# Convolution: the low parts of fourteen weights as a sign-turned cast plus an accumulating transfer

## The chip, the cores and the metric

The kernel runs on one core of a Trainium2 chip. Five engines work side by side, each through its own queue of instructions in a fixed order: TensorE (PE, matmuls), VectorE (DVE), ScalarE (ACT), GpSimd (POOL) and SyncE (SP, which here only issues transfers). They wait for each other and for transfers through semaphores. The metric is the device time in microseconds (us); three runs of the kernel before gave 1223.39, 1224.14 and 1225.11, so its time is their median, 1224.14 us.

## The reference, cut to what matters

Two decoder layers over 512 tokens of width 1024 in float32. The first layer begins with a causal convolution module, and only this stage is touched by the change:

```python
u = rms_norm(h, conv_norm_g)
a = u @ w_pw1 + b_pw1                               # 1024 -> 2048
u = a[..., :1024] * sigmoid(a[..., 1024:])          # value half, gate half
u = depthwise_conv(u, dw_w, width=31) + dw_b        # causal, per channel
u = silu(layer_norm(u, ln_g, ln_b))
h = h + u @ w_pw2 + b_pw2
# after it: the SwiGLU FFN, and h + sigmoid(rms_norm(h) @ ple_w_gate) * (p @ ple_w_proj);
# then the second layer with differential attention in place of the convolution
```

## The kernel before, in words

**Split operands.** To keep float32 precision, each operand of a matmul is split into a high part (`hi`, a rounded cast) and a low part (`lo = raw - hi`). A product is three matmuls, `mm3` (L182 to L185): low weight times high input first, then high times low, then high times high. A weight tile is 128 x 1024 (512 KB) and serves as eight 128 x 128 pieces, so half a chunk (one accumulator) takes 8 x 3 = 24 matmuls.

**Weights.** `weight` fetches a raw tile into `wraw`, a ring of two (L166, issued by SP), casts it on ACT into `whi` (L171) and subtracts on an engine `eng` into `wlo` (L173); `whi` and `wlo` are rings of four tiles, so two pairs. A weight's raw tile is free again once its last reader is done. I call the weights w0, w1, ... in the order in which they are fetched: w0 to w3 belong to chunks 0 and 1; w4 and w5 are gate and value of chunk 2, w6 and w7 of chunk 3, and so on to w14 and w15 of chunk 7. Two more, `pw`, serve the projections of `p` that fill PE after the convolution (`factor`, L617 and before). The low parts of w4 to w15 are DVE's, those of `pw` are POOL's.

**The loop over eight chunks of 128 channels.** For chunk c, PE makes the gate half, then the value half. Chunk 0 and 1 start before the norm is known: the row factors `rb` of the norm are multiplied in afterwards. `rb` comes from PE transposes (L263), is copied by ACT (L240), and DVE multiplies gate and value by it (L557, L559), which empties the PSUM accumulators, of which there are four (`mm`). ACT applies the sigmoid (L558), DVE joins both (L563, L575). The depthwise taps are made in two ways:

- Chunks 1, 3, 5, 6 ("phased"): the result is stored to DRAM (`pi`, L389, SP), read back rearranged by four transfers (`C`, L393, SP), multiplied on PE with diagonal matrices (L422, 64 matmuls of 128 x 128 per chunk, diagonals `D` and `C` loaded by SP at L406 and L412), copied out by ACT (L435), stored (`po`, L437, issued by ACT for chunks 1 and 3) and read back by four transfers (`B`, L440, SP), and finished on DVE (L449).
- Chunks 0, 2, 4, 7: some taps are products on ACT (L475, into four tiles in turn) added by POOL (L476), the others run on DVE (L487), with a last sum on DVE (L492).

Then the moments for the layer norm are formed (L515, L520, L523, L595) and turned by PE transposes (L256) and a spread (L263). Chunk 0's ones-matmul (L513) gives a per-token shift that is taken off early.

**What sets the order.** The kernel is written as one program and a scheduler fixes each engine's order statically; a few steps are tied by hand (`issue_after`). An instruction that waits holds up all that stands behind it on the same engine, and SP's and POOL's transfers too.

Of the kernel before, what the change touches and what calls it, by code (L numbers as in the profile page):

```python
# [13 lines left out]
F32R = mybir.dt.float32r  # L14
AF = mybir.ActivationFunctionType
ALU = mybir.AluOpType
# [43 lines left out]
BEHIND = (6,)  # L60
# [34 lines left out]
def trunk(ctx, tc, xT, pT, wts, diag, dww, vec, rel, lamv, out):  # L95
    nc = tc.nc
    V, A, G, T = nc.vector, nc.scalar, nc.gpsimd, nc.tensor
# [7 lines left out]
    def sb(shape, tag, bufs, dt=F32):  # L105
        uid[0] += 1
        return pool.tile(shape, dt, tag=tag, name=f"{tag}_{uid[0]}", bufs=bufs)
# [17 lines left out]
    def col(name, i=0):  # L125
        a, _ = VEC[name]
        return vt[:, a + i : a + i + 1]
# [22 lines left out]
    def opened(homes=None, raw_home=None):  # L150
        i = wnext[0]
        wnext[0] += 1
        if raw_home:
            raw = sb([P, 2, S], raw_home, 1).rearrange("p a s -> p (a s)")
        else:
            raw = sb([P, 1024], "wraw", 2)
        if homes:
            hi, lo = (sb([P, 2, S], t, 2, F32R).rearrange("p a s -> p (a s)") for t in homes)
        else:
            hi, lo = (sb([P, 1024], t, 4, F32R) for t in ("whi", "wlo"))  # L160
        return i, raw, hi, lo

    def fetch(w, cut, behind=None):
        i, raw, _, _ = w
        with tc.issue_after(behind.ins) if behind else nullcontext():
            loaded[0] = nc.sync.dma_start(raw[:, cut], wts[i, :, cut])  # L166

    def parts(w, cut, eng=V, after=None, behind=None):
        _, raw, hi, lo = w
        with tc.issue_after(behind.ins) if behind else nullcontext():  # L170
            last_cast[0] = A.copy(hi[:, cut], raw[:, cut])  # L171
        with tc.issue_after(after.ins) if after else nullcontext():
            eng.tensor_tensor(lo[:, cut], raw[:, cut], f(hi[:, cut]), ALU.subtract)  # L173

    def weight(n=1024, home=None, load_behind=None, **how):
        w, cut = opened(home), slice(0, n)
        fetch(w, cut, load_behind)
        parts(w, cut, **how)
        return w[2:]
# [90 lines left out]
    pairs = [(w1[2:], w0[2:]), (w3[2:], w2[2:])]  # L270
# [28 lines left out]
    def pfeatures(layer, parts, behind=None):  # L299
        for k, (hi, lo) in enumerate(parts):  # L300
            if layer == 0:
                if k == 0:
                    two = sb([P, 2, S], "B7", 1)
                    with tc.issue_after(loaded[0].ins):
                        nc.sync.dma_start(two.rearrange("p a s -> p (a s)"), pT[layer])
                raw = two[:, k]
            else:
                raw = sb([P, 1024], "wraw", 2)[:, :S]
                nc.sync.dma_start(raw, pT[layer, :, k * S : (k + 1) * S])
            with tc.issue_after(behind.ins) if behind else nullcontext():  # L310
                A.copy(hi, raw)
            (G if layer == 0 else V).tensor_tensor(lo, raw, f(hi), ALU.subtract)
        return parts
# [25 lines left out]
    phase_load = [None]  # L339
# [3 lines left out]
    def half(w, behind={}):  # L343
        acc = mm()
        held = nullcontext
        for k in range(NC):
            if k in behind:
                held = partial(tc.issue_after, behind[k].ins)
            with held():
                mm3(acc, wpart(w, k), norm.u[k], k == 0, k == NC - 1)  # L350
        return acc

    def first_halves(wa, wg):
        pg, pa = mm(), mm()
        for k in range(NC):
            (uh, ul), last = norm.u[k], k == NC - 1
            for acc, w in ((pg, wg), (pa, wa)):
                wh, wl = wpart(w, k)
                T.matmul(acc, wh, uh, start=k == 0, stop=False)
                T.matmul(acc, wl, uh, start=False, stop=False)  # L360
            for acc, w in ((pg, wg), (pa, wa)):
                T.matmul(acc, wpart(w, k)[0], ul, start=False, stop=last)
        return pg, pa

    def wt(c, j):
        return dwt[:, c * KW + j : c * KW + j + 1]
# [4 lines left out]
    def pe_taps(c):  # L371

        acc = accs[c] = sc() if c < NC - 2 else mm()
        if c in PHASED:
            return phased_taps(c, acc)
        for j in range(PE_TAPS[c]):
            if j % 4 == 0:
                n = min(4, PE_TAPS[c] - j)
                dg = sb([P, 2, 4, P], "C5", 2)[:, 0]
                with tc.issue_after(outs[NC - 3].ins):  # L380
                    nc.sync.dma_start(dg[:, :n], diag[TAPS.index((c, j)), :, :n])
            if j == 0:
                T.matmul(acc, ident, shrow, start=True, stop=False)
            last_tap[0] = T.matmul(acc, dg[:, j % 4], ups[c][:, j : j + S], start=False, stop=(j == PE_TAPS[c] - 1))

    def phased_in(c, src):

        d = dram.tile([P, S], F32, tag=f"pi{c}", name=f"pi{c}")
        nc.sync.dma_start(d, src)  # L389
        xs = ups[c] = sb([P, NPH, LEAD + P], "C1", 2)  # L390
        G.memset(xs[:, :, :LEAD], 0.0)
        for i in range(NPH):
            phase_load[0] = nc.sync.dma_start(  # L393
                xs[i * FG : (i + 1) * FG, :, LEAD:],
                bass.AP(d.tensor, d.offset + i * P, [[S, FG], [FG * S, NPH], [1, P]]),
            )
# [138 lines left out]
    for c in range(NC):  # L535
        wa, wg = pairs[c]
        if c == 0:
            pg, pa = first_halves(wa, wg)
            norm.factors()
            rb = norm.rows()  # L540
            pairs.append((weight(), weight())[::-1])
            pair_loads.append(loaded[0])
            ph = pfeatures(0, [(sb([P, S], t, 2, F32R), sb([P, S], t, 2, F32R)) for t in ("wth", "wtl")], norm.spread)
        if 1 < c < NC - 1:
            pairs.append((weight(), weight(load_behind=phase_load[0] if c + 1 in BEHIND else None))[::-1])
            pair_loads.append(loaded[0])
        if c > 0:
            pg = half(wg)
            if c - 1 not in PHASED:
                pe_taps(c - 1)  # L550
            pa = half(wa, {1: norm.last_column, 6: norm.last_row} if c == 1 else {})
            if c - 1 in PHASED and c < NC - 2:
                pe_taps(c - 1)
            if c == NC - 1:
                pe_taps(c - 2)
        tg, ta = big(), big()
        V.tensor_tensor(tg, pg, rb, ALU.mult)  # L557
        A.activation(tg, tg, AF.Sigmoid, bias=col("b_pw1", 8 + c))  # L558
        V.tensor_tensor(ta, pa, rb, ALU.mult)  # L559
        if c in PHASED:  # L560
            up = big()
            phases, tok = "p (r n) -> p n r", "p (n r) -> p n r"
            V.scalar_tensor_tensor(  # L563
                up.rearrange(phases, r=NPH), ta.rearrange(tok, r=NPH), col("b_pw1", c),
                tg.rearrange(tok, r=NPH), ALU.add, ALU.mult,
            )
            phased_in(c, up)
            rest = rests[c] = sb([P, 2, P], "rest", 2)[:, :, : P - LAGS]
            old = up.rearrange("p (r n) -> p r n", r=NPH)[:, :, : P - LAGS]
            A.activation(rest, old[:, 2:], AF.Copy, scale=wt(c, 0))  # L570
            V.scalar_tensor_tensor(rest[:, 0], old[:, 3], wt(c, 1), rest[:, 0], ALU.mult, ALU.add)
        else:
            up = ups[c] = sb([P, S + PAD], "C0", 2)
            G.memset(up[:, :PAD], 0.0)
            V.scalar_tensor_tensor(up[:, PAD:], ta, col("b_pw1", c), tg, ALU.add, ALU.mult)  # L575
        if c == NC - 1:
            other_taps(c - 2)
            pe_taps(c - 1)
        if c > 0 and c != NC - 2:
            other_taps(c - 1)  # L580
        if c == 1:
            moments(0)
        elif c > 3:
            moments(c - 3)
# [36 lines left out]
            held.append(copy)  # L621
        pp.append(o)

    pw = [weight(eng=G), weight(eng=G)]
    vs = sb([P, P // 2], "v8", 2)[:, :12]
    for m in range(4):
        factor(last_tap, bank=(mm, mm, mm, sc)[m])
# [566 lines left out]
    for m in range(NC):  # L1194
        if m % 4 == 0:
            w = weight()
# [154 lines left out]
```

## Time and profile before

| | |
|---|---|
| median of three runs | 1224.14 us |
| the profiled execution's own time | 1225.47 us |
| its span (first to last instruction) | 1223.7 us |
| PE busy in the span | 1215.3 us, 99% |
| DVE / ACT / POOL busy | 897.1 / 623.2 / 279.3 us |
| transfers issued by SP, ACT (q1, q10) / by POOL (q0) | 139.0 MB / 16.78 MB |

The profiled execution is one run, 1.33 us above the median. A row of a group reads: line, engine, operation, output<-inputs, shapes, count, then the busy time and the mean of one in ns, then the engine's idle time just before and what ended most of it. In rows of a timeline the first two numbers are the start and the length in us, and the square bracket tells what the engine had waited for. A row of transfers has the size of each and the median time from issue to landing. A name such as `wlo<-wraw,whi` gives output and inputs without buffer numbers.

### The profile page before, as it was taken

The page shows a single profiled execution, that of the slowest core. Times are in us where ns is not written, and L with a number is a line of the kernel's source. Part 1 is how long each engine was busy: PE and PEld are TensorE (multiplying, and loading weights), DVE is VectorE, ACT ScalarE, POOL GpSimd, SP SyncE. Part 2 cuts the span into 40 slices and gives each one's busy share as a digit, 9 for nine tenths or more (in the row PEclk, how much of TensorE's full clock was granted, in tenths as well). Part 3 has the DMA queues.
Part 4 walks back from the last instruction along what each step waited for, and adds up shares of the span by engine and source line. Part 5 has one row for each costly group of instructions (what it writes and reads, how often), then busy time and mean ns, then how long its engine had stood idle before and what let it go on. Part 6 is the DMA issues. An engine that isn't in the chain of part 4 may idle for free.

```text
span 1223.7 us, 18446 instructions
## 1 busy us (share of the span) xinstructions
PE 1215.3 (99%) x7080; PEld 1072.7 (88%) x7080; DVE 897.1 (73%) x1442; ACT 623.2 (51%) x1039; POOL 279.3 (23%) x238
## 2 busy tenths in 40 slices
PE   9999999999999999999999999999999999999998
PEld 7888788898999899888888989888898999899887
DVE  6999957965698458668668879647865687568668
ACT  6764645432355235446566779635442355235443
POOL 0879421000000000042626544131000000000120
PEclk9999999999999999999999999999999999999999
DMA  8655232663567444243222214412654577353241
GB/s 285 216 177 157 93 121 71 187 165 111 125 170 185 141 106 123 84 145 96 76 92 78 78 55 128 138 59 79 182 163 122 136 173 190 105 138 94 78 139 69
DMA packets 60056, 156.96 MB, mean 128 GB/s; under 512 B 6336, under 2 KB 11200, under 8 KB 59968
## 3 DMA queue, kind: packets, MB, share of 16 engines
q1 hardware_dynamic: 53632, 136.20, 34.9%
q0 software_dynamic: 4608, 16.78, 8.3%
q10 hardware_dynamic: 1728, 2.80, 0.8%
q8 instruction: 55, 0.90, 0.3%
q14 instruction: 33, 0.27, 0.1%
HBM read 150.52 MB, written 4.19 MB: 126 GB/s over the span
## 4 chain that ended last, share of the span: by engine, by line
PE 88%; DVE 5%; DMA 3%; issue 1%; POOL 1%; ACT 1%; SPq 0%; DVEq 0%; POOLq 0%; ACTq 0%
PE mm L183 23%; PE mm L184 23%; PE mm L185 23%; PE tp L185 2%; PE tp L184 2%; PE tp L183 2%; PE sc L184 2%; PE sc L185 2%; PE sc L183 2%; PE mm L1119 1%; DVE wlo L173 1%; DMA C<-in_wts 1%; POOL wk L476 1%; DVE sc L487 1%; DMA wraw<-in_wts 1%
## 5 line engine op out<-in xcount | busy, mean ns | idle before, releaser
L183 PE MATMUL mm<-A,wlo 128*128 128x512 f32 (+1 forms) x816 | 277.0, 342 | 0.5 <-DVE wlo L775 0.5
L184 PE MATMUL mm<-A,whi 128*128 128x512 f32 (+1 forms) x816 | 276.8, 340 | 0.5 <-DVE A L198 0.5
L185 PE MATMUL mm<-A,whi 128*128 128x512 f32 (+1 forms) x816 | 276.9, 340 | 0.0
L171 ACT CAST whi<-wraw 128x1024 fp32r<-128x1024 f32 (+2 forms) x142 | 143.4, 1019 | 206.3 <-PE mm L185 88.1
L173 DVE TENSOR_TENSOR wlo<-wraw,whi 128x1024 fp32r<-128x1024 f32 (+2 forms) x135 | 171.7, 1275 | 54.5 <-ACT whi L171 54.4
L183 PEld LDWEIGHTS mm<-A,wlo 128*128 128x128 f32 x816 | 154.8, 190 | 18.1 <-PE sc L185 0.6
L184 PEld LDWEIGHTS mm<-A,whi 128*128 128x128 f32 x816 | 154.8, 190 | 17.7 <-DVE A L198 0.9
L185 PEld LDWEIGHTS mm<-A,whi 128*128 128x128 f32 x816 | 154.8, 190 | 16.6
L184 PE MATMUL mm<-B,whi 128*128 128x512 f32 (+1 forms) x384 | 147.5, 385 | 0.0
L185 PE MATMUL mm<-B,whi 128*128 128x512 f32 (+1 forms) x384 | 147.4, 385 | 0.0
L183 PE MATMUL mm<-B,wlo 128*128 128x512 f32 (+1 forms) x384 | 145.3, 386 | 0.0
L782 POOL DMA_DIRECT2D C<-in_wts x32 | 27.9, 873 | 506.3 <-DVE h L893 134.8
L224 POOL TENSOR_TENSOR acc<-acc,wk 128x512 f32<-128x512 f32 x34 | 55.8, 1640 | 215.3 <-ACT wk L222 107.4
L185 PEld LDWEIGHTS mm<-B,whi 128*128 128x128 f32 x384 | 72.1, 188 | 14.4
L183 PEld LDWEIGHTS mm<-B,wlo 128*128 128x128 f32 x384 | 72.2, 188 | 13.9
L184 PEld LDWEIGHTS mm<-B,whi 128*128 128x128 f32 x384 | 72.2, 188 | 13.7
L184 PE MATMUL mm<-wlo,A 128*128 128x512 f32 (+1 forms) x224 | 81.6, 367 | 0.0
L183 PE MATMUL mm<-whi,A 128*128 128x512 f32 (+1 forms) x224 | 80.9, 366 | 0.0
L185 PE MATMUL mm<-whi,A 128*128 128x512 f32 (+1 forms) x224 | 80.4, 362 | 0.0
L893 DVE TENSOR_TENSOR h<-mm,h 128x512 f32<-128x512 f32 x48 | 32.9, 687 | 63.5 <-PE mm L185 63.5
L250 POOL TENSOR_TENSOR r<-v,mhalf 128x8 f32<-128x8 f32 (+1 forms) x30 | 45.3, 1511 | 123.3 <-DVE v L248 122.5
L476 POOL TENSOR_TENSOR wk<-wk,C 128x512 f32<-128x512 f32 x43 | 63.4, 1479 | 13.5 <-ACT C L475 10.8
(322 smaller groups left out, 2749.6 us busy)
## 6 DMA issues: line engine op xcount, KB each, us to landing
wraw<-in_wts SPq DMA_DIRECT2D x161, 512.0 KB, 3.7
C<-in_wts SPq DMA_DIRECT2D x32, 512.0 KB, 4.5
C<-in_wts POOLq DMA_DIRECT2D x32, 512.0 KB, 6.0
bias<-in_wts SPq DMA_DIRECT2D x32, 256.0 KB, 3.3
wraw<-in_wts SPq DMA_DIRECT2D x16, 384.0 KB, 3.1
D<-in_diag SPq DMA_DIRECT2D x18, 256.0 KB, 4.9
C<-in_diag SPq DMA_DIRECT2D x15, 256.0 KB, 5.6
h<-in_xT SPq DMA_DIRECT2D x8, 256.0 KB, 5.2
```

The lines of the kernel that those rows point to most:

```text
L171: last_cast[0] = A.copy(hi[:, cut], raw[:, cut])
L173: eng.tensor_tensor(lo[:, cut], raw[:, cut], f(hi[:, cut]), ALU.subtract)
L183: T.matmul(acc, al, bh, start=first, stop=False)
L184: T.matmul(acc, ah, bl, start=False, stop=False)
L185: return T.matmul(acc, ah, bh, start=False, stop=last)
L224: self.last = eng.tensor_tensor(self.acc, self.acc, sq, ALU.add)
L250: last_pow[0] = G.tensor_tensor(r[:, :n], v[:, :n], mhalf[:, :n], ALU.pow)
L476: last_pool[0] = G.tensor_tensor(pacc, pacc, pr, ALU.add)
L487: last_sum = V.scalar_tensor_tensor(sum_, tap(j), wt(c, j), sum_, ALU.mult, ALU.add)
L782: nc.gpsimd.dma_start(q, wts[i + 2].rearrange("p (a s) -> p a s", a=2), accum_op=ALU.add)
L893: V.tensor_tensor(h[m], acc, h[m], ALU.add)
L1119: T.matmul(o, wt[:, k * P : (k + 1) * P], val[hd, k], start=(k == 0), stop=(k == qb))
```

## The change

For w4 to w15 and the two `pw` weights the subtract is replaced. ACT casts the raw tile into `whi` as before, and then writes `-hi` into `wlo`; POOL issues a transfer that reads the raw weight a second time from DRAM and adds it onto `wlo` as it lands, so `wlo = -hi + raw`. w0 to w3 and all later weights keep their subtract.

```diff
@@ def parts(w, cut, eng=V, after=None, behind=None):
             last_cast[0] = A.copy(hi[:, cut], raw[:, cut])
+        if eng is None:
+            A.activation(lo[:, cut], hi[:, cut], AF.Copy, scale=-1.0)
+            nc.gpsimd.dma_start(lo[:, cut], wts[w[0], :, cut].bitcast(F32R), accum_op=ALU.add)
+            return
         with tc.issue_after(after.ins) if after else nullcontext():
             eng.tensor_tensor(lo[:, cut], raw[:, cut], f(hi[:, cut]), ALU.subtract)
@@ for c in range(NC), c == 0:
-            pairs.append((weight(), weight())[::-1])
+            pairs.append((weight(eng=None), weight(eng=None))[::-1])
@@ 1 < c < NC - 1:
-            pairs.append((weight(), weight(load_behind=phase_load[0] if c + 1 in BEHIND else None))[::-1])
+            pairs.append((weight(eng=None), weight(eng=None, load_behind=phase_load[0] if c + 1 in BEHIND else None))[::-1])
@@ after the loop
-    pw = [weight(eng=G), weight(eng=G)]
+    pw = [weight(eng=None), weight(eng=None)]
```

Since the scheduler orders the program anew, other instructions move with it, all of them in the convolution stage. The line numbers of the changed kernel are higher by 4 from L175 on; its sign-turned cast is L173, its accumulating transfer L174.

On ACT, around the copy of the row factors `rb`. Before; `whi_269`, `whi_275`, `whi_425` are w4, w5, w6, and `wth`, `wtl` the split `p`:

```order
L171 CAST whi_269<-wraw_268 128x1024
L171 CAST whi_275<-wraw_274 128x1024
L240 COPY rb_261<-tp_262 128x512
L311 CAST wth_280<-B_72_284 128x512
L311 CAST wtl_282<-B_72_284 128x512
L171 CAST whi_425<-wraw_424 128x1024
L558 ACT_TABLE_LOAD
```

The change, with w4, w5 and w6 now 269, 276 and 427, and their low parts 270, 277 and 428:

```order
L171 CAST whi_269<-wraw_268 128x1024
L173 ACTIVATE wlo_270<-whi_269 128x1024
L171 CAST whi_276<-wraw_275 128x1024
L173 ACTIVATE wlo_277<-whi_276 128x1024
L171 CAST whi_427<-wraw_426 128x1024
L173 ACTIVATE wlo_428<-whi_427 128x1024
L244 COPY rb_261<-tp_262 128x512
L315 CAST wth_282<-B_72_286 128x512
L315 CAST wtl_284<-B_72_286 128x512
L562 ACT_TABLE_LOAD
```

The cast of w6 stood behind the `rb` copy and stands ahead of it now, followed by its sign-turned cast. On SP, w6's raw tile has likewise moved, from behind four diagonals (`D`) to ahead of them.

On POOL, between the norm's power (`r_59`) and chunk 0's adds (`wk_367`, then `wk_369`). Before:

```order
L250 TENSOR_TENSOR r_59_259<-v_58_257,mhalf_71 128x4
L312 TENSOR_TENSOR wth_281<-B_72_284,wth_280 128x512
L312 TENSOR_TENSOR wtl_283<-B_72_284,wtl_282 128x512
L476 TENSOR_TENSOR wk_367<-wk_367,C_85_369 128x512
L476 TENSOR_TENSOR wk_367<-wk_367,C_86_372 128x512
L476 TENSOR_TENSOR wk_367<-wk_367,C_87_375 128x512
L476 TENSOR_TENSOR wk_367<-wk_367,C_88_378 128x512
L476 TENSOR_TENSOR wk_367<-wk_367,C_89_381 128x512
L476 TENSOR_TENSOR wk_367<-wk_367,C_90_384 128x512
```

The change (`wlo_435` is the low part of w7):

```order
L174 DMA wlo_270<-in_wts 128x1024
L174 DMA wlo_277<-in_wts 128x1024
L254 TENSOR_TENSOR r_59_259<-v_58_257,mhalf_71 128x4
L174 DMA wlo_428<-in_wts 128x1024
L316 TENSOR_TENSOR wth_283<-B_72_286,wth_282 128x512
L316 TENSOR_TENSOR wtl_285<-B_72_286,wtl_284 128x512
L480 TENSOR_TENSOR wk_369<-wk_369,C_85_371 128x512
L480 TENSOR_TENSOR wk_369<-wk_369,C_86_374 128x512
L480 TENSOR_TENSOR wk_369<-wk_369,C_87_377 128x512
L480 TENSOR_TENSOR wk_369<-wk_369,C_88_380 128x512
L480 TENSOR_TENSOR wk_369<-wk_369,C_89_383 128x512
L174 DMA wlo_435<-in_wts 128x1024
```

w7's accumulating transfer stands behind five of chunk 0's adds. Those of the next weights follow between the adds of chunks 0 and 2; w10's stands ahead of the third to fifth add of chunk 2 (`C_133` to `C_135` in the change), and ACT's copy of chunk 1's taps (L439) stands behind the product that takes the tile which the add of `C_135` frees.

On PE, chunk 1's taps (`sc_486`, in the change `sc_490`). Before, they stand inside the gate half of chunk 3 (w6, `wlo_426`):

```order
L185 MATMUL mm_564<-A_37_153,whi_425 128x512
L422 MATMUL sc_486<-C_82_358,D_105_487 128x128 x4
L422 MATMUL sc_486<-C_82_358,D_106_489 128x128 x4
L422 MATMUL sc_486<-C_82_358,D_107_491 128x128 x4
L422 MATMUL sc_486<-C_82_358,D_108_493 128x128 x4
L422 MATMUL sc_486<-C_82_358,C_109_495 128x128 x8
L422 MATMUL sc_486<-C_82_358,C_110_498 128x128 x8
L183 MATMUL mm_564<-A_39_157,wlo_426 128x512
```

The change: inside the value half (w7, `wlo_435`), behind ten of its matmuls:

```order
L187 MATMUL mm_596<-A_35_145,wlo_435 128x512
L426 MATMUL sc_490<-C_82_360,D_105_491 128x128 x4
L426 MATMUL sc_490<-C_82_360,D_106_493 128x128 x4
L426 MATMUL sc_490<-C_82_360,D_107_495 128x128 x4
L426 MATMUL sc_490<-C_82_360,D_108_497 128x128 x4
L426 MATMUL sc_490<-C_82_360,C_109_499 128x128 x8
L426 MATMUL sc_490<-C_82_360,C_110_502 128x128 x3
L517 MATMUL tp_421<-B_94_398,ones_70 128x512
L426 MATMUL sc_490<-C_82_360,C_110_502 128x128 x5
L188 MATMUL mm_596<-A_36_146,whi_434 128x512
```

The order counts each of these float32 matmuls once; the profile shows 64 for a chunk's 32. They moved back by some 20 matmuls, and the ones-matmul of chunk 0 went in among them. Chunk 3's taps likewise moved, from behind chunk 4's value half to behind six matmuls of chunk 5's gate half.

## The prediction

> **What bounds the kernel now.** I read the page's totals first, then the conv stage (the first 140 us) by windows, since the diff touches only weights of that stage, and last what TensorE (PE) waited for.
>
> ```profile
> span 1223.7 us, 18446 instructions
> PE 1215.3 (99%) x7080; PEld 1072.7 (88%) x7080; DVE 897.1 (73%) x1442; ACT 623.2 (51%) x1039; POOL 279.3 (23%) x238
> ```
>
> PE is busy 99% of the span. The windows show the stage of the change (columns: length; busy time of PE, PEld, DVE, ACT, POOL; granted clock; share of the DMA engines; GB/s):
>
> ```profile
> 20.00:136.70 116.70, 115.58 (x631) 97.84 (x630) 108.93 (x133) 66.60 (x97) 89.38 (x64) 1.00 0.57 187
> 20.00:30.00 10.00, 10.00 (x48) 7.94 (x47) 5.23 (x8) 3.14 (x5) 1.18 (x2) 1.00 0.86 303
> 30.00:45.00 15.00, 14.99 (x69) 12.46 (x69) 14.96 (x18) 13.96 (x20) 10.28 (x8) 1.00 0.68 225
> ```
>
> VectorE (DVE) is as full here as PE: 108.9 of 116.7 us against 115.6. This is where taking work from DVE could pay, and PE's waits in the first 260 us say how much:
>
> ```profile
> PE tp L256 <- DVE acc L523: 1.2, 1, 1.2
> PE tp L142 <- DVE wk L136: 1.1, 1, 1.1
> PE mm L359 <- ACT whi L171: 0.9, 1, 0.9
> ```
>
> The last two are the start-up, which the change leaves alone. The one wait for DVE is the 1.2 us before the transposes that end the conv stage, where the moments come late. DVE's load is otherwise hidden behind PE. So **the gain is capped near 1.2 us**, half of the 0.2% (2.45 us) that a measurement of this kernel tells from no change. Losses are not capped: PE has no slack here, and each late operand is paid in full.
>
> **The change, part by part.** Removed: twelve low-part subtracts on DVE and two on POOL. Added: fourteen sign-turned casts on ACT, and fourteen accumulating transfers issued by POOL.
>
> ```profile
> L173 DVE TENSOR_TENSOR wlo<-wraw,whi 128x1024 fp32r<-128x1024 f32 (+1 forms) x32 | 44.1, 1381 | 5.6 <-ACT whi L171 5.6
> L173 POOL TENSOR_TENSOR wlo<-wraw,whi 128x1024 fp32r<-128x1024 f32 x4 | 9.6, 2398 | 0.0
> L475 ACT ACTIVATE C<-C,C 128x512 f32<-128x512 f32 x43 | 29.5, 717 | 10.0 <-POOL wk L476 9.9
> L476 POOL TENSOR_TENSOR wk<-wk,C 128x512 f32<-128x512 f32 x43 | 63.4, 1479 | 13.5 <-ACT C L475 10.8
> ```
>
> DVE loses 12 x 1.381 = 16.6 us. The sign-turned cast is not in this trace. Two rows bound it: the plain cast of the same tile, 1.05 us (below), and twice a scaled copy of half the width, 2 x 0.717 = 1.43. It is a one-input pass with a constant scale, nearest to the cast: 1.05, so ACT gains 14.7 us. The trace has accumulating transfers of 512 KB, a later stage's, which are all that the software queue q0 moves:
>
> ```profile
> q1 hardware_dynamic: 53632, 136.20, 34.9%
> q0 software_dynamic: 4608, 16.78, 8.3%
> L782 POOL DMA_DIRECT2D C<-in_wts x32: 856/862/1053, 229.8 to 1104.5; - x32
> DMA to landing us min/median/max: 5.2/6.0/9.0
> ```
>
> Each costs POOL 0.862 us to issue: POOL gains 14 x 0.862 - 2 x 2.398 = 7.3 us. The second price is on the DMA engines: 8.3% of 1223.7 over 32 is 3.17 us of all engines each, where a plain 512 KB takes 34.9% x 1223.7 / (136.20 / 0.524) = 1.64. Fourteen add 44.4 us to a stage that has 0.57 x 116.7 = 66.5, so its share goes from 0.57 to about 0.95. The third price is latency. A low part now needs cast, sign-turned cast, issue and 5.2 to 9.0 us of landing, where a subtract of 1.4 us stood. I take **8.0 us** for landing, towards the upper end, because the engines will be nearly full. All else is a question of which PE operand comes too late, in order of time.
>
> *(a) The row factors `rb`.* ACT's timeline, two rows of SP's, and the DMA row of the transfer between (`pT`; KB, us to landing):
>
> ```profile
> 19.72 1.05 ACT L171 CAST whi<-wraw 128x1024 fp32r<-128x1024 f32 x1 [0.49 <-DMA wraw<-in_wts]
> 23.02 1.05 ACT L171 CAST whi<-wraw 128x1024 fp32r<-128x1024 f32 x1 [2.25 <-DMA wraw<-in_wts]
> 28.68 0.58 ACT L240 COPY rb<-tp 128x512 f32<-128x512 f32 x1 [4.61 <-PE tp L263]
> 30.37 1.05 ACT L171 CAST whi<-wraw 128x1024 fp32r<-128x1024 f32 x1
> ```
>
> ```profile
> 20.85 1.86 SPq L406 DMA_DIRECT2D D<-in_diag  x4
> 22.82 0.68 SPq L166 DMA_DIRECT2D wraw<-in_wts  x1
> ```
>
> ```profile
> B<-in_pT SPq DMA_DIRECT2D x1, 512.0 KB, 5.8
> ```
>
> The raw tile of chunk 3's gate weight (w6) moves ahead of the four diagonals on SP, to about 20.8, when the cast at 19.72 has freed its slot; its cast and its sign-turned cast move ahead of the `rb` copy on ACT. Behind the copy stand all sigmoids, and DVE's products with `rb`, which empty the PSUM banks that PE takes at 30.04 (the chain of waits):
>
> ```profile
> 30.04 0.49 PE mm L183
> ```
>
> The 512 KB issued just before it took 5.8 us in the window whose share is 0.86, and two accumulates of 3.17 us now share that window: I add a third of their 6.3 and let w6 land at 28.8 (26.6 without them, 29.8 with half). Cast and sign-turned cast end at 30.9, so the copy starts there instead of at 28.68: PE is held by **+2.2 us** (0 to 3.2). The first accumulate (w4, issue 19.72 + 2 x 1.05 = 21.8, landing 27.0 to 30.8) lies under this wait.
>
> ```profile
> 32.91 0.39 PE L183 MATMUL mm<-A,wlo 128*128 128x512 f32 x1
> 41.07 0.39 PE L183 MATMUL mm<-A,wlo 128*128 128x512 f32 x1
> 36.74 18.20 POOL L476 TENSOR_TENSOR wk<-wk,C 128x512 f32<-128x512 f32 x12 [4.33 <-ACT C L475]
> ```
>
> ```profile
> L476 POOL TENSOR_TENSOR wk<-wk,C x43: 1268/1298/2292, 36.7 to 129.6; 128x512 f32<-128x512 f32 x43
> ```
>
> *(b) The low part of w7.* From 32.91 to 41.07 PE issued 36 matmuls: 0.227 us each, 5.45 a half of 24. Chunk 2's matmuls start at 30.04 + 2.2 = 32.2, and w7 is needed three halves later, at 48.6. On POOL its accumulate stands behind five of the twelve adds that start at 36.74. That first add came 8.06 after the `rb` copy; with two casts gone from between (w6's ahead, w7's behind) it comes at 30.9 + 8.06 - 2.1 = 36.9. Five adds at 1.30 (the stage's median) to 1.52 (18.20 for 12, waits included) end at 43.4 to 44.5; from 43.8 with 8.0 of landing the low part is there at 51.8: **+3.2** (0 with landing 5.2; 4.9 with 44.5 and 9.0).
>
> *(c) Chunk 3's tap inputs.* In `before`:
>
> ```profile
> 44.63 5.37 PE sc L422 x48
> 54.22 0.57 ACT L435 COPY big<-sc 128x512 f32<-128x512 f32 x1
> 55.03 0.34 ACTq L437 DMA_DIRECT2D po<-big  x1
> 59.18 1.75 SPq L440 DMA_DIRECT2D B<-po  x4
> 64.30 0.34 SPq L389 DMA_DIRECT2D pi<-big  x1
> 66.30 2.00 SPq L393 DMA_DIRECT2D C<-pi  x4
> ```
>
> ```profile
> C<-pi SPq DMA_DIRECT2D x16, 64.0 KB, 2.0
> wraw<-in_wts SPq DMA_DIRECT2D x161, 512.0 KB, 3.7
> ```
>
> A tap matmul takes 5.37 / 48 = 0.112. Chunk 1's 64 taps now stand inside w7's half behind 10 of its matmuls, with the ones-matmul among them: 51.8 + 2.3 + 7.2 + 0.5 = 61.8, where they ended at 51.8 before. The copy of their result, its store `po`, four reads `B`, then chunk 3's `pi` and its four reads `C` follow one another on SP, so the copy sets chunk 3's inputs: 0.81 to the store, 4.15 to the reads, 1.75 for them, 2.0 to the `C` reads, 1.3 to the last of these and 2.0 to land, 12.0 in all, and 1.9 (a sixth) for crowded engines. The copy stands on ACT behind a product that waits for POOL's add of C_135; that add now has w10's accumulate ahead of it, which waits for w10's sign-turned cast. w10's raw tile takes w8's slot: about 49.5, landing 7 (3.7 is the median, against a full queue), then cast, two products and sign-turned cast, 3.5: 60.0. Issue, three adds and a product end at 60.0 + 0.9 + 4.5 + 0.7 = 66.1, and the inputs are there at 80.0. PE reaches these taps 68 matmuls after chunk 1's: 61.8 + 15.4 = 77.2. **+2.8**; nothing if POOL isn't held (62.6 + 12.0 = 74.6), 6.9 if the chain takes half as long again.
>
> *(d) The later weights* (w11 to the pair after the conv) go by the same queue, but further ahead of their use: 0 to one more wait like (b), 3.2; I take a third, **+1.0**. Outside (a) the sign-turned casts cost nothing, since PE's work covers ACT, busy 66.6 of 116.7 us; without that cover they would cost up to 14.7.
>
> *(e) The end of the stage.* DVE's 16.6 us come off ahead of the moments: **-1.2**, unless POOL's adds or a late chunk take their place (0).
>
> Sum: 2.2 + 3.2 + 2.8 + 1.0 - 1.2 = +8.0. The profiled execution took 1225.47 (span 1223.7), so the changed one takes 1233.5; the median of the runs shown, 1224.14, lies 1.33 lower, and so **1232.1**.
>
> **The rivals.** *Everything lands in time.* With landings at 5.2, (b) is 0; with no POOL hold, (c) is 0; (a) alone stays, or falls with w6 landing before 28. Between -1.2 and +2.2: 1223 to 1226. For it: the median landing is 6.0, and these transfers ran beside raw weights too. Against it: w6's two passes stand ahead of `rb` in any case, and the share of 0.95. Chance 0.14, and this is the case that ends not slower. [...]
>
> *The DMA engines saturate.* With 44.4 us in the first 116.7, and 20 to 30 us already at 0.86, queues build up: every landing is 9.0 or more, raw tiles and diagonals come late as well. Then (a) 3.2, (b) 4.9, (c) 6.9, (d) 3.2 without the gain: +18.2, about 1242. It decides from a share above 0.95 over a whole chunk. Chance 0.14.
>
> *It is only an order effect:* taps in another place, transfers hidden, (c) without the rest, +2.8 - 1.2: 1225.7. Against it: a raw tile and fourteen passes of ACT do move ahead of `rb` and of products. Chance 0.05.
>
> **How the numbers follow.** The forecast (several waits of 1 to 4 us each) has 0.67; its own range is 1227 to 1239, the sum with one term at nothing or one at its upper bound. With the rivals' parts the range is 1225 to 1243. Faster by over 0.2% (below 1221.7) needs more than PE's whole wait for DVE: 0.03, out of the first rival. Within 0.2%: 0.10 of the first rival, 0.03 of the third, 0.01 of the forecast, 0.14. Slower: the rest, 0.83.
>
> **What would show it.** Right: PE waits that name the accumulating transfer into `wlo`, one at the first matmul of w7's half of 2 to 5 us; the `rb` copy near 30.9 with PE idle before 32; a gap before chunk 3's taps that ends with reads of `pi`; DMA share near 0.9 from 20 to 137; no wait left at the transposes that end the stage; from there on, everything as before, moved. Wrong: landings of 5 to 6 in the crowded stretch and no wait at w7 would overturn (b) and the share that I count; PE waiting for POOL's adds or ACT instead would mean that the added instructions, not the transfers, set the pace.

## The result, and the profile after

The change made the kernel slower: 1242.62 us median of five runs (1241.8 to 1243.73) against 1224.21 us of the kernel before (five runs by now), a ratio of 1.0151 with a 95% interval of 1.0136 to 1.0166. The direction was forecast, the size was not: +18.4 us where +8.0 stood in the sum.

The totals of the changed kernel's page:

```profile
span 1242.0 us, 18476 instructions
PE 1223.3 (98%) x7080; PEld 1078.7 (87%) x7080; DVE 885.1 (71%) x1430; ACT 636.0 (51%) x1053; POOL 279.3 (22%) x250
```

The span grew by 18.3 us, and it splits in two. PE's idle time (span less busy) went from 1223.7 - 1215.3 = 8.4 to 1242.0 - 1223.3 = 18.7 us: **+10.3**. PE's busy time went from 1215.3 to 1223.3 with the same 7080 matmuls: **+8.0**. The second part has no counterpart in the prediction. DVE's busy time fell by 12.0 us (897.1 to 885.1), where 16.6 were worked out.

PE's waits in the first 280 us (in all, times, longest), and where four of them end on PE's timeline:

```profile
PE mm L187 <- DMA wlo<-in_wts: 5.1, 2, 3.0
PE sc L426 <- DMA C<-pi: 3.8, 1, 3.8
PE mm L426 <- DMA C<-in_diag: 3.3, 1, 3.3
...
PE mm L187 <- DVE sc L491: 0.9, 1, 0.9
```

```profile
32.41 0.77 PE L187 MATMUL mm<-A,wlo 128*128 128x512 f32 x1 [3.00 <-DMA wlo<-in_wts]
81.14 6.47 PE L426 MATMUL sc<-C,D 128*128 128x128 f32 x32 [3.84 <-DMA C<-pi]
119.44 0.47 PE L187 MATMUL mm<-A,wlo 128*128 128x512 f32 x1 [2.06 <-DMA wlo<-in_wts]
137.26 7.22 PE L426 MATMUL mm<-C,D 128*128 128x128 f32 x48 [3.32 <-DMA C<-in_diag]
```

They are the low part of w4, chunk 3's tap inputs, the low part of w15, and the diagonals of chunk 6. The wait of 0.9 stands at w7's first matmul; the profile names a DVE instruction for it. The wait for DVE before the closing transposes, 1.2 us before, is gone. Now the granted clock behind these waits (columns: length; busy time of PE, PEld, DVE, ACT, POOL; granted clock; DMA share; GB/s):

```profile
20.00:136.70 116.70, 104.14 (x528) 87.86 (x526) 84.21 (x104) 71.42 (x98) 78.41 (x68) 0.94 0.85 229
...
32.00:36.00 4.00, 3.59 (x10) 2.85 (x10) 3.38 (x6) 3.73 (x6) 1.83 (x3) 0.57 1.06 258
36.00:40.00 4.00, 4.00 (x19) 3.32 (x18) 1.66 (x3) 1.44 (x3) 3.77 (x4) 1.00 1.03 327
80.00:86.00 6.00, 4.86 (x23) 4.89 (x24) 5.86 (x9) 0.45 (x1) 1.26 (x1) 0.50 0.97 216
...
121.00:124.00 3.00, 3.00 (x9) 2.32 (x8) 1.43 (x3) 0.81 (x2) 2.20 (x3) 0.50 0.79 108
138.00:141.00 3.00, 3.00 (x16) 3.00 (x15) 2.46 (x4) 0.00 (x0) 2.84 (x3) 0.50 0.19 66
```

Behind each of the four waits PE runs at half its clock. In the 4 us from 32 it does 10 matmuls, in the 4 us from 36 it does 19. Traced in quarter microseconds, the half clock lies under PE's work for 3.1 us (32.41 to 35.5), 5.6 (81.14 to 86.7), 3.4 (120.9 to 124.3) and 3.4 (137.9 to 141.3). Half of these 15.5 us is 7.8, near the 8.0 by which the busy time grew. So the loss is waits plus the slow clock that follows them.

The transfers behind the waits, from the DMA part of the page, the line of the accumulating transfer, and the DMA issues of the first 160 us (KB each, median us to landing), with the diagonals' row of the kernel before last:

```profile
q0 software_dynamic: 6624, 24.12, 11.5%
```

```profile
DMA to landing us min/median/max: 5.4/8.5/10.2
```

```profile
D<-in_diag SPq DMA_DIRECT2D x18, 256.0 KB, 8.7
...
C<-pi SPq DMA_DIRECT2D x16, 64.0 KB, 4.3
```

```profile
D<-in_diag SPq DMA_DIRECT2D x18, 256.0 KB, 4.9
```

An accumulating 512 KB costs (11.5% x 1242.0 - 8.3% x 1223.7) / 14 = 2.9 us of all DMA engines, near the 3.17 that was used. Not only these transfers are slow: the diagonals take 8.7 us to land where the view of the kernel before has 4.9, and the `C` reads 4.3 where it has 2.0.

### The profile page after: what moved, and what is told of

Same layout as the page of the kernel before. It is cut to its first block, busy times and chain, and to the rows that moved or that the text cites. A ratio compares the mean times of both kernels' runs of the same rounds, so it can differ in the third digit from the quotient of the medians.

```text
span 1242.0 us, 18476 instructions
## 1 busy us (share of the span) xinstructions
PE 1223.3 (98%) x7080; PEld 1078.7 (87%) x7080; DVE 885.1 (71%) x1430; ACT 636.0 (51%) x1053; POOL 279.3 (22%) x250
## 3 DMA queue, kind: packets, MB, share of 16 engines
q0 software_dynamic: 6624, 24.12, 11.5%
## 4 chain that ended last, share of the span: by engine, by line
PE 89%; DMA 6%; ACT 2%; DVE 1%; issue 1%; SPq 0%; POOL 0%; ACTq 0%; POOLq 0%; DVEq 0%
PE mm L187 23%; PE mm L188 23%; PE mm L189 23%; PE tp L189 3%; PE tp L188 3%; PE tp L187 3%; DMA wraw<-in_wts 2%; PE sc L188 2%; PE sc L189 2%; PE sc L187 2%; PE mm L1123 1%; DMA D<-in_diag 1%; PE sc L1090 1%; PE sc L1089 1%; PE mm L426 1%
## 5 line engine op out<-in xcount | busy, mean ns | idle before, releaser
L177 DVE TENSOR_TENSOR wlo<-wraw,whi 128x1024 fp32r<-128x1024 f32 (+2 forms) x123 | 151.5, 1235 | 52.5 <-ACT whi L171 52.4
L480 POOL TENSOR_TENSOR wk<-wk,C 128x512 f32<-128x512 f32 x43 | 59.4, 1382 | 12.9 <-ACT C L479 11.0
```

Of the source, the lines that this page charges most:

```text
L480: last_pool[0] = G.tensor_tensor(pacc, pacc, pr, ALU.add)
```

## The experiments

Twelve kernels, each beside the kernel before on the same chip.

**The sign-turned casts without the transfers.** DVE (POOL for `pw`) adds the raw tile in place of the transfer; the order is nearly the change's.

```diff
             A.activation(lo[:, cut], hi[:, cut], AF.Copy, scale=-1.0)
-            nc.gpsimd.dma_start(lo[:, cut], wts[w[0], :, cut].bitcast(F32R), accum_op=ALU.add)
+            (G if w[0] > 15 else V).tensor_tensor(lo[:, cut], raw[:, cut], f(lo[:, cut]), ALU.add)
```

> The fourteen sign-turned casts on ACT stay, nearly in the order of the change, but the raw weight is added from its tile by DVE (twelve) and POOL (two); no accumulating transfer is left. Theory A (the loss comes from late transfers, as PE waits and as a TensorE clock of 0.50 in the windows behind a wait): no wait for wlo, DMA share of 20 to 137 us near 0.57, clock 1.00 throughout, 1224 to 1228 us. Rival B (the ACT work and the moved order are the price): 1234 us or more, with waits of PE that name ACT or DVE.

1226.42 us, ratio 1.0014 (1.0005 to 1.0024). The one wait beside the start-up, on its list:

```profile
PE mm L426 <- DMA D<-in_diag: 1.7, 1, 1.7
```

The clock is 1.00 in every window to 160 us. ACT's 14 casts and the moved order are worth some 1.8 us (2.9 at the interval's end); the other 15.5 to 16.6 come with the transfers. Rival B falls.

**Which weights.** One kernel keeps the subtract for w4 to w7, another uses the transfer for these four alone.

```diff
+        if eng is None and w[0] not in tuple(range(8, 18)):   # the other kernel: (4, 5, 6, 7)
+            eng = G if w[0] > 15 else V
         if eng is None:
```

> w4 to w7 keep the subtract on DVE, the other ten weights are as in the change. Theory A, where each wait stands by itself: the first wait (3.0 us, and half of 3.4 us of slow clock) and the 0.9 us at w7 vanish, those at chunk 3's taps, at w15 and at chunk 6's diagonals stay with their slow clock: 1233 to 1238 us. Rival C (the first four weights put SP's queue behind, and the later waits follow from that): the later waits shrink too, 1224 to 1229 us.

1229.75 us, ratio 1.0040 (1.0030 to 1.0050):

```profile
PE mm L428 <- DMA C<-in_diag: 3.8, 1, 3.8
PE mm L189 <- DMA wlo<-in_wts: 1.5, 1, 1.5
```

> Only w4 to w7 use the accumulating transfer, the other ten keep their subtract. Theory A: the first wait and its slow clock and the one at w7, 5 to 7 us: 1229 to 1232 us. Rival C: nearly the whole loss, 1236 us or more, with waits at chunk 3's taps and chunk 6's diagonals.

1232.2 us, ratio 1.0063 (1.0048 to 1.0078):

```profile
PE mm L189 <- DMA wlo<-in_wts: 4.3, 2, 2.3
PE mm L428 <- DMA D<-in_diag: 1.8, 1, 1.8
```

The first four cost 7.6 us alone, slightly more than A said, the other ten 5.2, less than A said and at the border of C. The wait at chunk 3's taps is in neither kernel, so it needs both parts; the one at chunk 6's diagonals is in both. The parts add to 12.8 of 18.4; the rest is what they do to each other. Neither A (each wait by itself) nor C (all from the first four) holds as it was put.

**Does the clock fall because PE waits?** Nine artificial waits in the two FFN stages of the kernel before. This kernel does extra work, so its total (1294.03 us) says nothing; the waits were longer than meant, since the chain also queued on DVE.

```diff
+    T.matmul(t1[:, 0:P], ident, ident, start=True, stop=True)
+    V.tensor_scalar(v_, t1[:, 0:4], 1.0, 1.0, ALU.mult, ALU.add)
+    # cnt times: G.tensor_tensor(r_, v_, mhalf[:, :4], ALU.pow)
+    go = T.matmul(t2[:, 0:4], ident, v_, start=True, stop=True)   # the next half issues behind it
```

> The kernel before with nine artificial waits of PE in the two FFN stages, each a chain matmul, DVE, 0 to 4 POOL powers, matmul (powers per place in order: 0, 2, 1, 3, 1, 3, 4, 2, 1), some 0.6 to 6 us long, with all else as before. Theory A: behind waits of about 2 us and more the granted clock is 0.50 for 3.4 us or a little longer, behind shorter ones it stays 1.00, so that five or six of the nine cost some 1.7 us beyond their own length; at these places the DMA share is low. Rival (the slow clock belongs to the crowded transfers, not to PE's wait): 1.00 behind all nine.

Seven of the nine (3.08 to 10.32 us long) have the clock at 0.50 behind them, 1.81 and 2.48 do not. Two places, by timeline and windows:

```profile
206.85 0.39 PE L882 MATMUL sc<-v,ident 128*128 128x4 f32 x2 [2.48 <-DVE v L876]
...
279.79 0.38 PE L882 MATMUL sc<-r,ident 128*128 128x4 f32 x2 [3.40 <-POOL r L879]
```

```profile
208.00:212.00 4.00, 4.00 (x20) 3.30 (x19) 4.00 (x7) 3.77 (x7) 0.00 (x0) 1.00 0.00 2
...
281.00:284.00 3.00, 3.00 (x9) 2.32 (x8) 0.00 (x0) 0.00 (x0) 0.00 (x0) 0.50 0.47 91
284.50:288.00 3.50, 3.50 (x20) 2.99 (x19) 0.58 (x1) 0.52 (x1) 0.00 (x0) 1.00 0.00 0
```

The slow clock comes with PE's waits in these stages too, and it came without a transfer beside it: in the wait of 8.12 us, which ends at 942.64, it falls at 939.5 while the DMA share is 0.00 (939.0 to 943.5), and behind the one of 7.59 it stays at 0.50 to 266.5 with a share of 0.00 from 262.0 on. The share was not low at every place, though, and an accumulating transfer of this stage was issued at 277.75, ahead of the wait that ends at 279.79. The length of the wait alone does not decide: 2.48 us went free here, 2.06 us in the changed kernel did not. What does decide was not shown; the last section has more such pairs.

**The change without `pw`.** w4 to w15 as in the change.

```diff
+        if eng is None and w[0] not in tuple(range(4, 16)):
+            eng = G if w[0] > 15 else V
```

> The change without the last two of its fourteen weights: the pair pw keeps its subtract on POOL, w4 to w15 use the accumulating transfer. Theory P (chunk 6's diagonals are late because POOL stood 2.9 us at pw's accumulate for its sign-turned cast, which made chunk 4's sum and chunk 6's product on DVE late, and with them the stores and diagonals on SP): the wait of 3.3 us and its window of slow clock vanish, 1236 to 1239 us. Rival (crowded transfers alone make them late): the wait stays above 2 us, 1241 to 1243.

1237.17 us, ratio 1.0103 (1.0086 to 1.0120), as P said. In the changed kernel the chain behind the diagonals reads, on POOL, DVE and SP:

```profile
120.24 0.88 POOL L174 DMA_DIRECT2D wlo<-in_wts  x1 [2.89 <-ACT wlo L173]
122.47 0.69 DVE L496 TENSOR_TENSOR B<-sc,wk 128x512 f32<-128x512 f32 x1 [4.29 <-POOL wk L480]
125.51 0.34 SPq L393 DMA_DIRECT2D pi<-big  x1
```

POOL stands for `pw`'s sign-turned cast, its next add is late, chunk 4's sum waits 4.29 us for that add, chunk 6's product and its store `pi` come behind it, and the diagonals stand behind `pi` on SP. Without `pw` the store comes at 121.71 and the wait for diagonals is gone; waits for low parts and for `C` reads remain:

```profile
PE mm L189 <- DMA wlo<-in_wts: 8.7, 4, 2.5
PE sc L428 <- DMA C<-pi: 1.9, 1, 1.9
```

The chain is not all of it, though. The rows of chunk 6's four `D` diagonals, in the kernel before, in the changed kernel and without `pw`:

```profile
D<-in_diag SPq DMA_DIRECT2D x4, 256.0 KB, 2.9
D<-in_diag SPq DMA_DIRECT2D x4, 256.0 KB, 6.3
D<-in_diag SPq DMA_DIRECT2D x4, 256.0 KB, 3.3
```

In the changed kernel the four are issued by 131.6, 2.3 us before PE is ready for the taps (133.9); in the other two kernels they are issued 3.05 us ahead of it. So the later issue cost some 0.8 us of lead, while the landing took 3.0 us longer than without `pw`. Leaving `pw` out takes away both the hold on POOL and the bytes of two transfers, so this run does not separate them.

**PE kept busy while it waits.** The changed kernel plus matmuls that nobody reads, twelve ahead of w4's half and eight ahead of w15's.

```diff
+    def fill(n):
+        t, (uh, _) = tp(), norm.u[0]
+        with tc.issue_after(last_half[0].ins):
+            for _ in range(n):
+                last = T.matmul(t, uh[:, :P], uh, start=True, stop=True)
+        return last          # the half's own matmuls issue behind it
```

> The change with idle matmuls that nobody reads, twelve of 0.23 us ahead of w4's half and eight ahead of w15's, in the two places where PE waited 3.0 and 2.1 us for a low part. Theory A (the clock falls because PE stands still): the granted clock stays at 1.00 behind both, PE reaches the next chunk 1.7 us earlier at each; up to 3.4 us less, 1239 to 1241 us, or 1241 to 1243 where the next wait, set by transfers and other engines, takes it back. Rival (crowded transfers or the accumulates themselves go with the slow clock): 0.50 behind both places as before.

1235.57 us, ratio 1.0087 (1.0072 to 1.0102): some 7 us less than the change, with more work for PE. The windows that had 0.57 and 0.50:

```profile
32.00:36.00 4.00, 4.00 (x19) 3.32 (x18) 3.72 (x5) 3.72 (x7) 1.76 (x3) 1.00 1.07 248
...
121.00:124.00 3.00, 3.00 (x18) 2.57 (x18) 0.49 (x1) 0.72 (x1) 3.00 (x3) 1.00 0.81 132
```

The DMA share is as high as before (1.07), the clock is full: it is the standing still. That the gain exceeds 3.4 us is not all the clock's. Some instructions moved on ACT, POOL and PE, and the wait at the diagonals is gone while the one at chunk 3's taps grew to 4.8 us; what of the 7 us belongs to this was not separated.

**Half the columns.** The transfer and the sign-turned cast for 512 columns, the old subtract for the other 512.

```diff
-            A.activation(lo[:, cut], hi[:, cut], AF.Copy, scale=-1.0)
-            nc.gpsimd.dma_start(lo[:, cut], wts[w[0], :, cut].bitcast(F32R), accum_op=ALU.add)
-            return
+            eng = G if w[0] > 15 else V
+            A.activation(lo[:, S:], hi[:, S:], AF.Copy, scale=-1.0)
+            nc.gpsimd.dma_start(lo[:, S:], wts[w[0], :, S:].bitcast(F32R), accum_op=ALU.add)
+            cut = slice(0, S)
```

> The change for one half of the columns of each of the fourteen weights; the other half is subtracted by DVE (POOL for pw) as before. Half the bytes are read again, the number of issues on POOL stays. Theory D: landings of 5 to 7 us, waits cut by more than half and mostly under 2 us, so that the clock holds: 1227 to 1233 us. Rival (the number of POOL issues and their holds set the waits): 1236 us or more.

1236.65 us, ratio 1.0096 (1.0081 to 1.0111): a miss for D, at the border of the rival. The waits are fewer and late in the stage, and the clock is at 0.50 beside two of them, from 117.0 to 120.5 us behind 1.90 us for `C` reads and from 127.3 to 134.1 around 3.01 us for diagonals:

```profile
PE mm L427 <- DMA D<-in_diag: 3.0, 1, 3.0
PE sc L427 <- DMA C<-pi: 2.5, 2, 1.9
```

Half the bytes saved little more than a third of the loss (11.6 us above the kernel before, for 18.4). This kernel has both ways of making a low part and an order of its own, so it left the question between bytes and holds open.

**Load without a chain, twice tried.** First, fourteen DRAM-to-DRAM copies added to the kernel before.

```diff
+        if 3 < w[0] < 18:
+            with tc.issue_after(last_cast[0].ins):
+                nc.gpsimd.dma_start(dram.tile([P, 1024], F32, ...), wts[w[0]])
```

> The kernel before, every subtract in place, plus fourteen copies of the same raw weights from DRAM to DRAM that POOL issues behind the casts of the same fourteen weights and nobody waits for. Theory D (crowding of the DMA engines is enough): raw tiles, diagonals and C reads land later, PE waits at two or three places, 1229 to 1238 us. Rival L (it is the longer chain to a low part, cast, sign-turned cast, issue, landing): DMA share rises, PE hardly waits, 1224 to 1227 us.

1263.3 us, ratio 1.0311 (1.0295 to 1.0326), and inconclusive: the hand-set order is no wait, so POOL issued all the copies in the first 20 us (24 instructions there, 10 in the kernel before), and PE lost most in the first 60 us, of which it was busy 33.8 for 58.0, while `h` took 23.3 us to land for 5.2 and the first weights (256 KB) 18.2 for 5.2. Then a store that depends on the cast, added to the kernel of the first experiment:

```diff
+            twice = dram.tile([P, 2, 1024], F32, ...)
+            nc.gpsimd.dma_start(twice, f(hi).unsqueeze(1).to_broadcast([P, 2, 1024]))
             (G if w[0] > 15 else V).tensor_tensor(lo[:, cut], raw[:, cut], f(lo[:, cut]), ALU.add)
```

> The kernel of the run with sign-turned casts and adds by DVE and POOL (which took 1226.4 us and whose DMA share of 45 to 60 us was 0.78), plus, at the place where the change issues each accumulating transfer, a store of the weight's high part to DRAM, twice over (1 MB), that nobody waits for. DMA time like the accumulate's, POOL issues in its place, no chain behind it. Theory D (crowding and holds on POOL make other transfers and products late): PE waits for raw parts, diagonals or C reads, 1231 us or more. Rival L (only the chain to the low part costs): 1226 to 1229 us.

1244.36 us, ratio 1.0157 (1.0142 to 1.0173); one of its four runs took 4291.86 us, for which no cause was found, and the others 1243.22 to 1245.06. Its longest wait (8.35 us, at `C` reads) goes with another order on SP, where chunk 5's reads had moved behind chunk 6's store. Not clean either: it fits D, and does not show it.

**`pw` alone.** The smallest use of the change, and the one that could have gained.

```diff
+        if eng is None and w[0] not in (16, 17):
+            eng = G if w[0] > 15 else V
```

> Only the last two of the fourteen weights use the accumulating transfer. The DMA share there (112 to 137 us) was 0.52 before, POOL is relieved of two subtracts of 2.4 us at the end of the stage. Theory A: no wait above 2 us; at most the 1.2 us before the closing transposes are gained: 1222.8 to 1224.5 us. Rival (POOL's hold for pw's sign-turned cast delays chunk 4's sum and the diagonals of chunk 6 here too): a wait of 1 to 3 us at chunk 6's taps, 1226 to 1229 us.

1230.33 us, ratio 1.0044 (1.0031 to 1.0058). One wait, and on SP the store `pi` of chunk 6 with its reads:

```profile
PE mm L428 <- DMA C<-in_diag: 4.5, 1, 4.5
```

```profile
107.73 0.34 SPq L395 DMA_DIRECT2D pi<-big  x1
112.86 3.08 SPq L399 DMA_DIRECT2D C<-pi  x4
```

`pi` is issued when it was before (107.75), but its reads follow 5.1 us later, where it took 2.0. The second `pw` transfer was issued at 106.43. Both expectations missed: theory A had no wait, and the rival had a shorter one (1 to 3 us) that came from a late store, while here the store is on time and its landing is late.

**The same transfers with an eighth of the bytes.** Each accumulating transfer covers 128 of 1024 columns, in all fourteen weights, and in `pw` alone (there the order is the same on every engine). The other columns stay `-hi`, so these two kernels leave out seven eighths of those low parts.

```diff
-            nc.gpsimd.dma_start(lo[:, cut], wts[w[0], :, cut].bitcast(F32R), accum_op=ALU.add)
+            nc.gpsimd.dma_start(lo[:, :P], wts[w[0], :, :P].bitcast(F32R), accum_op=ALU.add)
```

> The change with each of its fourteen transfers cut to 128 of 1024 columns (64 KB); for the other columns the low part stays -hi, so this kernel leaves out the rest of the low parts. The sign-turned casts, the fourteen issues on POOL and, but for some adds and a few matmuls, the order are those of the change. Theory D (the bytes make everything late): DMA share of 20 to 137 us near 0.6, no wait of 2 us, clock 1.00, 1223 to 1228 us. Rival H (POOL's holds and the ACT work): a wait at chunk 6's diagonals of 2 to 3 us stays and its slow clock, 1230 us or more.

1225.54 us, ratio 1.0010 (1.0000 to 1.0019), with fourteen casts, fourteen issues and their holds in place. The longest wait beside the start-up, the window of the stage, and the landing of a 64 KB transfer:

```profile
PE sc L426 <- DMA C<-pi: 1.3, 1, 1.3
```

```profile
20.00:136.70 116.70, 115.24 (x629) 97.45 (x628) 96.07 (x121) 79.36 (x112) 89.25 (x76) 1.00 0.64 195
```

```profile
wlo<-in_wts POOLq DMA_DIRECT2D x14, 64.0 KB, 3.0
```

> The kernel where only pw uses the transfer (1230.3 us, 4.5 us of wait at chunk 6's diagonals), order the same on all engines, the two transfers cut to 128 of 1024 columns (64 KB); the other columns of pw's low part stay -hi, so that part is left out. Theory D (the store pi of chunk 6 and its reads stood behind pw's transfer in the DMA engines): the C reads come 2 us after pi instead of 5.1, the wait falls under 2 us, clock 1.00: 1223 to 1226 us. Rival H (holds and order): the wait stays, 1229 to 1231 us.

1224.81 us, ratio 1.0005 (0.9996 to 1.0015):

```profile
107.91 0.34 SPq L395 DMA_DIRECT2D pi<-big  x1
110.27 1.73 SPq L399 DMA_DIRECT2D C<-pi  x4
```

```profile
PE mm L428 <- DMA D<-in_diag: 1.6, 1, 1.6
```

`pi` lands in 2.4 us again and the wait falls to 1.6, and the clock is 1.00 over the whole stage (20 to 136.7 us, 0.97 with the whole transfers). Here nothing but the bytes of two transfers changed, and 5.1 us came back, each kernel taken against its own kernel before (5.6 and 0.5 us above it). Together the two settle what the half left open: the bytes are the cause. Fewer bytes made the transfer itself land sooner (3.0 us for 8.5) and the transfers beside it too (the diagonals 4.5 for 8.7, the `C` reads 2.1 for 4.3); the run with all fourteen does not separate these, and in `pw` alone, where no low part was waited for, it is the second. The holds on POOL and the longer chain, by themselves, cost 1.3 us (2.3 at the interval's end); that they cost more once the transfers are slow is read from the chain above and not measured alone. No version beat the kernel before.

## Why the prediction was wrong in size, point by point

**The cap on the gain** was right: the wait of 1.2 us at the transposes went, and the kernel with an eighth of the bytes, whose DVE is relieved just as much, was no faster than the kernel before.

**The prices** were right: the sign-turned cast measured 1.04 us (1.05 taken), the issue 0.878 (0.862), the DMA time 2.9 (3.17), the landing 8.5 in the median (8.0). The share from 20 to 136.7 us was 0.85, not 0.95, since the stage itself took longer. The upper bound of a landing, 9.0, was passed: w4's took 10.2.

**(a) The first wait** came where it was put, with 3.0 us for 2.2, but for another reason. The casts of w6 on ACT:

```profile
27.62 1.05 ACT L171 CAST whi<-wraw 128x1024 fp32r<-128x1024 f32 x1 [2.54 <-DMA wraw<-in_wts]
28.70 1.06 ACT L173 ACTIVATE wlo<-whi 128x1024 fp32r<-128x1024 f32 x1
29.66 0.57 ACT L244 COPY rb<-tp 128x512 f32<-128x512 f32 x1
```

w6 landed at 27.6 (28.8 taken), `rb` was copied at 29.66 (30.9), and its products would have let PE go on at about 31. What PE waited for until 32.41 was the accumulate of w4, which the prediction laid under the wait for `rb` with a landing of at most 9.0.

**(b) w7** waited 0.85 us, not 3.2. Its low part was there at 51.2, just before PE went on at 51.30 and near the 51.8 worked out, but PE itself came 1.9 us later than assumed (50.45 for 48.6), held up by (a) and by the slow clock behind it. Here the wait that came first took from the one behind it.

**(c) Chunk 3's inputs** were there at 81.14 (80.0), a wait of 3.84 (2.8), but not by the path that was worked out. The copy of chunk 1's taps on ACT, and the transfers behind it:

```profile
62.76 0.57 ACT L439 COPY big<-sc 128x512 f32<-128x512 f32 x1
65.98 0.33 ACTq L441 DMA_DIRECT2D po<-big  x1
72.88 0.44 SPq L393 DMA_DIRECT2D pi<-big  x1
77.36 1.99 SPq L397 DMA_DIRECT2D C<-pi  x4
```

The copy came at 62.76, where the prediction had 66.1 with POOL held and 62.6 without: POOL stood only 1.74 us at w10's accumulate. From the copy to the inputs it then took 18.4 us, for 12.0 and 1.9 of crowding: the store `po` was issued 3.2 us behind the copy (0.81 taken), and the reads of `pi` came 4.5 us behind their store (2.0). The delay was in the transfers and not in POOL's hold, and that the two sizes nearly agree is luck.

**(d)** The later weights cost 2.06 at w15 (1.0).

These sum to 3.0 + 0.85 + 3.84 + 2.06 - 1.2 = 8.6 us of waits, where 8.0 stood. The forecast of the waits it knew was thus nearly right in all, in part by luck: (a) and (c) came by another path, and (b) came 2.4 us short and the other three 2.9 over. It was wrong by two terms that it left out, the clock (8.0) and one more wait (3.3). With that wait the sum is 11.9; PE's idle time grew by 10.3, because 0.7 us went at the start-up and 0.9 behind 160 us. The forecast's own range, 1227 to 1239, is also wider than its rule: one term at nothing or one at its upper bound makes 1229 to 1236.

**The step that failed** is the sum itself: it let PE go on at full speed after each wait, "Sum: 2.2 + 3.2 + 2.8 + 1.0 - 1.2 = +8.0". The slow clock added 8.0 us. The trace of before couldn't show it, since its longest wait of PE was 1.2 us and its clock 1.00; the forecast's own waits, 2.2 to 3.2 us, were longer than any there, and were priced as if nothing came behind them. The traces of the changed kernel show the clock at 0.50 behind waits of 2.06 to 3.84 us.

**The other term left out** is chunk 6's diagonals, 3.3 us. The saturation rival named late diagonals as a mishap but gave them no price. The chain behind them was of a kind that (c) had worked out for chunk 1's copy (POOL standing at an accumulate, an add late, a transfer late on SP), where it hardly came. It was not followed to chunk 6, where in the kernel before the four `D` diagonals were issued by 114.8 and the taps began at 117.8. The larger part of this wait, though, is their landing, 6.3 us for 2.9.

**The saturation rival** gave 1242, and 1242.6 came, but by other terms: its four waits sum to 18.2, measured waits gave 10.3 and the clock 8.0, so that the number agrees by luck. Its condition, a share above 0.95 over a whole chunk, was met twice, with 1.05 from 27 to 40 us and 1.06 from 52 to 63. Not every landing came to 9.0 (5.4 at the least). Its cause, more bytes than the DMA engines move in time, is the one that the eighths bear out.

## What to carry to other kernels

Here a transfer that replaced a vector instruction was paid for by the transfers beside it: before adding bytes to a stage, look up which small stores and loads stand on the path there, and what a later landing of each would cost. A late operand of PE can cost more than its wait: in the changed kernel the half clock added 1.7 us (half of 3.4) behind the wait of 2.06 and 2.8 (half of 5.6) behind that of 3.84, while waits of 2.48 in two other runs went free, so read the granted clock behind each wait. Twelve and eight matmuls that nobody reads, put in two of the waits, kept the clock at 1.00 here. Where an in-order engine issues transfers behind something it must wait for, follow what stands behind that wait to the end, chunk by chunk.

## What the runs showed of the hardware that was not expected

**The granted clock halves by some waits of PE, and not by others as long.** Six of the runs, with their waits of PE of 1.2 us and more, in us (the clock read in quarter-microsecond windows, for the casts without transfers in windows of 2 and 4 us):

| run | clock falls to 0.50 | clock stays at 1.00 |
|---|---|---|
| the change | 2.06, 3.00, 3.32, 3.84 | |
| nine artificial waits | 3.08, 3.40, 3.73, 7.59, 8.12, 8.89, 10.32 | 1.81, 2.48 |
| without `pw` | 1.83, 1.97 | 1.87, 2.45, 2.48 |
| the first four weights | 2.26 | 1.84, 2.07 |
| half the columns | 1.90, 3.01 | 1.52 |
| casts without transfers | | 1.68 |

Waits from 1.83 to 2.48 us stand on both sides, so something other than their length decides there, and the runs do not show what it is.

**The fall and the wait do not end together.** In the changed kernel the clock falls at 32.1, 79.9, 120.9 and 137.9 us, and the waits beside it end at 32.41, 81.14, 119.44 and 137.26: it fell inside two of them and 1.5 and 0.6 us behind the other two. The slow work behind the wait of 3.00 us, 3.1 us, was shorter than the 5.6 behind that of 3.84, and no run shows what sets how long it lasts.
